# Two reorderings in a two-layer trunk: the sum of the A11 and A12 products behind that of S2, and a tile's square ahead of its multiplication by the norm weights

## The chip, the cores and the metric

The kernel runs on one core of a Trainium2 chip. The metric is the device time of one launch in microseconds; shown are the median, the lowest and the highest of three runs. One more execution is recorded by the hardware profiler, and everything that is read from a trace comes from that one. TensorE is called PE here, VectorE DVE, ScalarE ACT, GpSimd POOL, and SyncE, which issues the transfers of this kernel, SP. Each engine works through its own list of instructions in order; between engines, semaphores make an instruction wait.

## The reference

`x` is 1024 tokens by 1024 features in float32. There are two layers, each with a mixer and a feed-forward block, each normed before and after:

```
for layer in range(2):
    h = rmsnorm(x, norm_mix_pre[layer])
    m = attention_mixer(h, ...) if layer == 0 else recurrent_mixer(h, ...)   # both end in "... @ w_out"
    x = x + rmsnorm(m, norm_mix_post[layer])
    h = rmsnorm(x, norm_ffn_pre[layer])
    f = (silu(h @ w_gate) * (h @ w_up)) @ w_down          # 1024 -> 2816 -> 1024
    x = x + rmsnorm(f, norm_ffn_post[layer])

rmsnorm(x, g) = x * rsqrt(mean(x * x) + 1e-6) * g
```

The change touches two places: the products of `h` with `w_gate` and `w_up`, and the norm of `m` behind the mixer's output product.

## The kernel before, in words

Every float32 operand is split into a high part (a cast, done by ACT) and a low part (the operand less its high part, done by DVE). A product is made of three matmuls: high by high, high by low, low by high.

**Stages.** Attention runs up to 512 us of the profiled execution, its output product (`out_product`) to 609, the gate and up products of layer 0 (`gate_up`) to 1044, its down product to 1268, the recurrent mixer to 1492, its output product to 1589, `gate_up` of layer 1 to 2024, and the down product to the end.

**Gate and up.** Each product by 256 weight columns is a block, done in the Strassen-Winograd way with seven products of half size, A11, A12, S2, S3, S1, S4 and A22 in this order on PE. Each is 12 matmuls of 128x512 (three for each of four 128-row parts), so a block is 84. Eleven gate blocks and eleven up blocks alternate in each layer (the first half of the first gate block runs inside the output product's end). `strassen` writes one block. Its sums come from PSUM: P1 (the A11 product) is copied to SBUF by ACT (L651); then DVE adds the A12 product to it (L653, the output tile c11), the S2 product to it (L654, u2), the S3 product to u2 (L655, u3), the S1 product to u2 and to u3 (L657, L659), the S4 product to u2 (L660), and subtracts the A22 product (L661). Products take turns on six PSUM tiles, each taking the one that is freed first, and so on into the next block: the A22 product takes the tile that P1's copy frees, and the first, second and third product of the next block take those that the first, second and third sum of this one free (L653, L654, L655). So a sum that is late on DVE makes PE wait some products later.

**Loading the weights.** `gate_load` brings the weights of one block in two tiles called `raw`, of 512 KB each: the A half (a11 and a21) and the B half (a12 and a22). There are three `raw` tiles, so a half can only be asked for (L599, on SP's queue) when the half three before it has been read for the last time. For the A half that last reading is the low part of S4 of the load two before; for the B half it is the low part of S3 of the load just before. ACT scales a half by the norm's weights (L602, four pieces of 128x256); then A11, A12 and A22 are split (cast L614 on ACT, low part L615 on DVE), DVE forms S2, S1, S3 and S4 in place (L621, L622, L623, L628), and these are split too. After a gate block ACT applies the silu (L693); after an up block DVE multiplies the two and forms sums for the down product (L698 to L704), which SP stores (L707).

**The output product's norm.** `out_product` treats the 1024 tokens as eight tiles, three, three and two at a time, and leaves each result in PSUM, 128 by 1024. `post_norm_of` then multiplies it by the norm weights into SBUF (DVE, L248), squares and sums it (ACT, L178), lets POOL form the reciprocal root (L182, L183), and DVE adds to the residual (L254). Behind that comes the next norm: a square of `x` (ACT, L178), two steps on POOL, a scaling (ACT, L212), and eight transposes on PE (L222), whose results are split into the operand `hS` of the gate and up products. The last two tiles, 6 and 7, end inside the first gate products. ACT and DVE read the same PSUM tile, and the framework lets one of them wait for the other, in the order of the program text.

**What sets the order.** The framework simulates the program with its own costs before it is built, and fixes each engine's list by that. The text of the kernel gives dependences and priorities, not the list itself; a line that is moved can reorder instructions well away from it.

Of the kernel before, what the change touches and what calls it, by code (L numbers as in the profile page):

```python
# [12 lines left out]
ALU = mybir.AluOpType  # L13
# [14 lines left out]
def rows(t, x):  # L28

    if not isinstance(t, tuple):  # L30
        return [(slice(0, P), x[t * P:(t + 1) * P, :])]
    r, a = t
    o = [2 * a * P + k * P + 64 * r for k in range(2)]
    return [(slice(64 * k, 64 * k + 64), x[o[k]:o[k] + 64, :]) for k in range(2)]
# [65 lines left out]
class Trunk:  # L100
# [134 lines left out]
    def post_norm_of(self, ms, mg, x_src, x_dst, t, gpost, sink, pool, x=None):  # L235

        nc = self.nc
        if x is None:  # L240
            x = pool.tile([P, D], F32, tag="nx", bufs=2, name=self.uid("x"))
        for d, s in rows(t, x_src):
            self.load(x[d, :], s)
        junk = pool.tile([P, D // len(ms)], BF16, tag="junk", bufs=1, name=self.uid("junk"))
        if mg is ms[0][1]:
            rs = self.rstd(pool, [m for _, m in ms], junk)
        for c, m in ms:
            scaled = nc.vector.tensor_tensor(mg[:, c], m, gpost[:, c], op=ALU.mult).ins  # L248
        if mg is not ms[0][1]:
            rs = self.rstd(pool, [m for _, m in ms], junk)  # L250
        self.last_m = [self.squared, scaled]

        def rest(later=False):
            nc.vector.scalar_tensor_tensor(x, mg, rs, x, op0=ALU.mult, op1=ALU.add)  # L254
            for k, (d, s) in enumerate(rows(t, x_dst)):
                (nc.scalar if k and sink is None else nc.sync).dma_start(s, x[d, :])
            if sink is not None:
                return self.pre_norm(pool, x, mg, None, sink, t, self.psum_t, later)

        return rest  # L260
# [211 lines left out]
    def psum(self):  # L472
        return self.pp.tile([P, 512], F32, tag="mm", bufs=6, name=self.uid("ps"))
# [158 lines left out]
    def strassen(self, hS, psum, c, q, cols, behind=()):  # L632

        nc = self.nc
        c11, u2, u3, c22 = c

        def product(name, i):
            ps, a = psum(), q[name]  # L640
            for kt in range(4):
                bh, bl = hS.op(i, 0, kt, cols), hS.op(i, 1, kt, cols)
                with self.behind(behind):
                    nc.tensor.matmul(ps, a[:, 0, kt, :], bh, start=kt == 0, stop=False)  # L644
                nc.tensor.matmul(ps, a[:, 0, kt, :], bl, start=False, stop=False)  # L645
                self.matmul = nc.tensor.matmul(ps, a[:, 1, kt, :], bh, start=False, stop=kt == 3).ins  # L646
            return ps

        tt = nc.vector.tensor_tensor
        p1 = c22  # L650
        nc.scalar.copy(p1, product("A11", 0))  # L651
        yield self.matmul
        tt(c11, product("A12", 1), p1, op=ALU.add)  # L653
        tt(u2, product("S2", 4), p1, op=ALU.add)  # L654
        tt(u3, product("S3", 5), u2, op=ALU.add)  # L655
        p5 = product("S1", 3)
        tt(u2, p5, u2, op=ALU.add)  # L657
        yield self.matmul
        tt(c22, p5, u3, op=ALU.add)  # L659
        tt(u2, product("S4", 2), u2, op=ALU.add)  # L660
        tt(u3, u3, product("A22", 6), op=ALU.subtract)  # L661

    def gate_up(self, ap, hS, early, wg, wu, gain, gO):
# [17 lines left out]
        for j in range(NF // 2):  # L681
            if j == 0:
                cg = blocks()
                strassen([o[:, late] for o in cg], q, late)
                for i, o in enumerate(cg):
                    nc.scalar.activation(o[:, early], first[:, i], AF.Silu)
                    nc.scalar.activation(o[:, late], o[:, late], AF.Silu)
            else:
                q = self.gate_load(ap, wg, gain, j, ["w"] * 7, self.last if j == 1 else None)
                cg = blocks()  # L690
                strassen(cg, q, full)
                for o in cg:
                    nc.scalar.activation(o, o, AF.Silu)  # L693
            qu = self.gate_load(ap, wu, gain, j, ["w"] + ["w2"] * 6, hS.last if j == 0 else None)
            cu = blocks()
            strassen(cu, qu, full)
            for o, u in zip(cg, cu):
                tt(o, u, o, op=ALU.mult)  # L698
            a11, a21, a12, a22 = cg
            s1, s2, s4, _ = cu  # L700
            tt(s1, a21, a22, op=ALU.add)
            tt(a21, a11, a21, op=ALU.subtract)
            tt(s2, s1, a11, op=ALU.subtract)
            tt(s4, a12, s2, op=ALU.subtract)  # L704
            for name, o in (("A11", a11), ("S2", s2), ("S3", a21), ("S1", s1), ("A22", a22),
                            ("S4", s4), ("A12", a12)):
                nc.sync.dma_start(gO[name][:, j] if name == "A12" else gO[name][j], o)  # L707
# [419 lines left out]
```

## Time and profile before

| | us |
|---|---|
| median of three runs | 2259.44 |
| lowest and highest | 2258.71, 2262.77 |
| profiled execution, its own time | 2258.71 |
| span of its trace | 2256.9 |
| PE busy | 2205.0 |
| DVE busy | 1547.2 |
| ACT busy | 1143.2 |
| POOL busy | 227.6 |

The granted TensorE clock was 0.994 of full speed on average. How to read rows: `L615 DVE TENSOR_TENSOR q<-raw,q` is a DVE instruction of kernel line 615 that writes a tile named `q` from tiles named `raw` and `q`; "[4.01 <-ACT q L614]" says that its engine stood idle for 4.01 us before it, and that the last thing it waited for was ACT's line 614. SPq is SP's queue; a row there is the time at which a transfer was issued, not how long it took. PE's records overlap: the duration of a matmul is longer than the distance to the next one.

### The profile page before, as it was taken

The numbers are of one execution on the slowest core, as the hardware profiler recorded it, in microseconds if no ns is written. First come the engines' busy times: TensorE is split into PE (matmuls) and PEld (weight loads), VectorE is DVE, ScalarE is ACT, GpSimd is POOL, SyncE is SP. The second block draws the span as 40 slices with busy tenths as digits, with TensorE's granted clock in tenths as the row PEclk, the third lists the DMA queues.
The fourth block names the chain that finished last, engine by engine and source line by source line (L and its number), as shares of the span: only waits on it lengthen the run. The fifth ranks groups of instructions, "written<-read, shape, count | busy, mean of one in ns | idle before, by whom it ended". The sixth has DMA issues, their size and how long they took to land. (4 is left out here: it accounts for less than half of the span.)

```text
span 2256.9 us, 30747 instructions
## 1 busy us (share of the span) xinstructions
PE 2205.0 (98%) x11198; PEld 1806.0 (80%) x11198; DVE 1547.2 (69%) x2496; ACT 1143.2 (51%) x2108; POOL 227.6 (10%) x458
## 2 busy tenths in 40 slices
PE   8999999999999999999999999999999999999997
PEld 8887888878788887778887777887788887788875
DVE  5776765464877767676867677437777667669665
ACT  4545455465765444442536676538754443425433
POOL 2111212131100000000001233102000000000011
PEclk9999999999999999999999999999999999999998
DMA  5101011125423323226558421356243322337466
GB/s 166 48 29 34 24 43 46 54 98 184 170 85 98 117 94 104 92 97 227 173 157 261 132 65 39 106 189 227 66 131 94 117 87 92 102 127 270 131 202 189
DMA packets 185977, 268.92 MB, mean 119 GB/s; under 512 B 13793, under 2 KB 115169, under 8 KB 185826
## 3 DMA queue, kind: packets, MB, share of 16 engines
q1 hardware_dynamic: 185186, 264.86, 37.3%
q10 hardware_dynamic: 640, 2.10, 0.3%
q8 instruction: 88, 1.44, 0.3%
q14 instruction: 63, 0.52, 0.1%
HBM read 201.38 MB, written 65.54 MB: 118 GB/s over the span
## 5 line engine op out<-in xcount | busy, mean ns | idle before, releaser
L644 PE MATMUL ps<-hS,q 128*128 128x512 f32 (+1 forms) x1288 | 492.8, 383 | 9.1 <-DVE c L655 4.3
L645 PE MATMUL ps<-hS,q 128*128 128x512 f32 (+1 forms) x1288 | 489.5, 380 | 1.4 <-DVE hS L89 1.4
L646 PE MATMUL ps<-hS,q 128*128 128x512 f32 (+1 forms) x1288 | 488.5, 380 | 0.0
L615 DVE TENSOR_TENSOR q<-raw,q 128x512 fp32r<-128x512 f32 x308 | 207.9, 687 | 206.7 <-ACT q L614 205.7
L644 PEld LDWEIGHTS ps<-hS,q 128*128 128x128 f32 x1288 | 241.7, 188 | 66.5 <-DVE c L659 8.1
L645 PEld LDWEIGHTS ps<-hS,q 128*128 128x128 f32 x1288 | 242.3, 188 | 47.2 <-DVE hS L89 1.8
L646 PEld LDWEIGHTS ps<-hS,q 128*128 128x128 f32 x1288 | 242.2, 188 | 46.3
L602 ACT ACTIVATE raw<-raw,gcol 128x256 f32<-128x256 f32 x352 | 151.9, 499 | 207.2 <-DMA raw<-in_ffn_w_gate_dram 95.0
L614 ACT CAST q<-raw 128x512 fp32r<-128x512 f32 x308 | 176.8, 614 | 147.9 <-DVE raw L623 145.0
L730 PE MATMUL ps<-o,o 128*128 128x512 f32 x616 | 241.8, 393 | 2.6 <-DVE o L725 2.6
L731 PE MATMUL ps<-o,o 128*128 128x512 f32 x616 | 239.4, 393 | 0.0
L729 PE MATMUL ps<-o,o 128*128 128x512 f32 x616 | 221.6, 394 | 9.4 <-ACT o L840 7.4
L724 ACT CAST o<-raw 128x512 fp32r<-128x512 f32 x206 | 123.2, 620 | 187.4 <-PE ps L731 54.3
L182 POOL TENSOR_SCALAR rs<-ss 128x1 f32<-128x1 f32 x60 | 34.8, 581 | 1468.5 <-ACT junk L178 1401.7
L725 DVE TENSOR_TENSOR o<-raw,o 128x512 fp32r<-128x512 f32 x206 | 137.6, 687 | 61.6 <-ACT o L724 60.8
L729 PEld LDWEIGHTS ps<-o,o 128*128 128x128 f32 x616 | 116.1, 189 | 38.0 <-ACT o L840 9.9
L156 DVE TENSOR_TENSOR wlo<-raw,whi 128x1024 fp32r<-128x1024 f32 x76 | 93.0, 1224 | 71.3 <-ACT whi L155 70.4
L730 PEld LDWEIGHTS ps<-o,o 128*128 128x128 f32 x616 | 116.7, 189 | 28.3 <-DVE o L725 4.3
L731 PEld LDWEIGHTS ps<-o,o 128*128 128x128 f32 x616 | 116.8, 190 | 25.0 <-DVE o L841 0.9
L155 ACT CAST whi<-raw 128x1024 fp32r<-128x1024 f32 x76 | 79.7, 1050 | 57.1 <-PE ps L167 20.2
L399 ACT COPY pt<-tr 128x512 f32<-128x512 f32 (+1 forms) x128 | 65.5, 527 | 79.6 <-PE tr L395 79.0
L166 PE MATMUL psq<-hT,whi 128*128 128x512 f32 x256 | 101.2, 395 | 1.1 <-DVE v L294 1.1
(201 smaller groups left out, 4306.8 us busy)
## 6 DMA issues: line engine op xcount, KB each, us to landing
raw<-in_ffn_w_down_dram SPq DMA_DIRECT2D x96, 256.0 KB, 4.4
raw<-in_ffn_w_gate_dram SPq DMA_DIRECT2D x44, 512.0 KB, 4.2
raw<-in_ffn_w_up_dram SPq DMA_DIRECT2D x44, 512.0 KB, 3.9
gS<-c SPq DMA_DIRECT2D x88, 256.0 KB, 2.3
raw<-gS SPq DMA_DIRECT2D x88, 256.0 KB, 2.8
gA<-c SPq DMA_DIRECT2D x66, 256.0 KB, 2.9
raw<-in_attn_w_in_dram SPq DMA_DIRECT2D x24, 512.0 KB, 4.1
raw<-gA SPq DMA_DIRECT2D x44, 256.0 KB, 2.7
```

The lines of the kernel that those rows point to most:

```text
L166: nc.tensor.matmul(ps, wh[:, kt, cols], hh[:, kt, :], start=kt == 0, stop=False)
L602: nc.scalar.activation(raw[:, i], raw[:, i], AF.Copy, scale=gain[:, 4 * k + i:4 * k + i + 1])
L614: self.last = nc.scalar.copy(t[:, 0], src).ins
L615: self.last_lo = nc.vector.tensor_tensor(t[:, 1], src, t[:, 0].bitcast(F32), op=ALU.subtract).ins
L644: nc.tensor.matmul(ps, a[:, 0, kt, :], bh, start=kt == 0, stop=False)
L645: nc.tensor.matmul(ps, a[:, 0, kt, :], bl, start=False, stop=False)
L646: self.matmul = nc.tensor.matmul(ps, a[:, 1, kt, :], bh, start=False, stop=kt == 3).ins
L724: nc.scalar.copy(t[:, 0], src)
L725: tt(t[:, 1], src, t[:, 0].bitcast(F32), op=ALU.subtract)
L729: nc.tensor.matmul(ps, a[0], b[:, 0], start=first, stop=False)
L730: nc.tensor.matmul(ps, a[0], b[:, 1], start=False, stop=False)
L731: nc.tensor.matmul(ps, a[1], b[:, 0], start=False, stop=last)
```

## The change

In `strassen`, the tile of P1 is now the one that becomes c11 (now called `s1`), no longer that of c22. The sum u2 of the S2 product and P1 is written first; the sum of the A12 product and P1 follows behind it, in place. In `post_norm_of`, where a tile comes in one part, the square now stands ahead of the multiplication; of the two readers of the PSUM tile, the multiplication is now the one that comes second.

```diff
@@ post_norm_of
-        if mg is ms[0][1]:
+
+        squares_first = mg is ms[0][1] or len(ms) == 1
+        if squares_first:
             rs = self.rstd(pool, [m for _, m in ms], junk)
         for c, m in ms:
             scaled = nc.vector.tensor_tensor(mg[:, c], m, gpost[:, c], op=ALU.mult).ins
-        if mg is not ms[0][1]:
+        if not squares_first:
             rs = self.rstd(pool, [m for _, m in ms], junk)
@@ strassen
-        c11, u2, u3, c22 = c
+        s1, u2, u3, c22 = c
...
         tt = nc.vector.tensor_tensor
-        p1 = c22
-        nc.scalar.copy(p1, product("A11", 0))
+        nc.scalar.copy(s1, product("A11", 0))
         yield self.matmul
-        tt(c11, product("A12", 1), p1, op=ALU.add)
-        tt(u2, product("S2", 4), p1, op=ALU.add)
+        p2 = product("A12", 1)
+        tt(u2, product("S2", 4), s1, op=ALU.add)
+        tt(s1, p2, s1, op=ALU.add)
         tt(u3, product("S3", 5), u2, op=ALU.add)
```

Lines behind the first edit are two further down in the changed kernel: the cast is L616, the low part L617, the scaling L604. Behind the second edit u2 is L655, s1 L656, u3 L657.

The fixed lists of the engines differ in more than these lines. First ACT's list in layer 0, over the stretch that the prediction reads from 941 to 961 us. Before: `raw_9579` and `raw_9585` are the A and the B half of a load; `q_9447` to `q_9453` are the seven operands of the load ahead of it, `q_9448` its A12, `q_9453` its A22, `q_9451` its S1, `q_9452` its S4.

```order
L614 CAST q_9448<-raw_9441 128x512
L693 ACTIVATE c_9173<-c_9173 128x512
L602 ACTIVATE raw_9579<-raw_9579,gcol 128x256 x4
L614 CAST q_9453<-raw_9441 128x512
L614 CAST q_9449<-raw_9435 128x512
L614 CAST q_9450<-raw_9435 128x512
L693 ACTIVATE c_9176<-c_9176 128x512
L614 CAST q_9451<-raw_9441 128x512
L693 ACTIVATE c_9174<-c_9174 128x512
L602 ACTIVATE raw_9585<-raw_9585,gcol 128x256 x2
L614 CAST q_9452<-raw_9441 128x512
```

Of the change, the same place:

```order
L604 ACTIVATE raw_9579<-raw_9579,gcol 128x256 x4
L616 CAST q_9448<-raw_9441 128x512
L616 CAST q_9453<-raw_9441 128x512
L695 ACTIVATE c_9173<-c_9173 128x512
L616 CAST q_9449<-raw_9435 128x512
L616 CAST q_9450<-raw_9435 128x512
L695 ACTIVATE c_9176<-c_9176 128x512
L616 CAST q_9451<-raw_9441 128x512
L695 ACTIVATE c_9174<-c_9174 128x512
L616 CAST q_9452<-raw_9441 128x512
L604 ACTIVATE raw_9585<-raw_9585,gcol 128x256 x4
```

The cast of S4 (`q_9452`) moved from behind the first two pieces of the B half's scaling to ahead of it; the cast of A12 (`q_9448`) moved from ahead of the A half's scaling to behind it.

DVE's list at the same place, before (`c_9173` to `c_9176` are the block's four output tiles):

```order
L615 TENSOR_TENSOR q_9447<-raw_9435,q_9447 128x512
L653 TENSOR_TENSOR c_9173<-ps_9191,c_9176 128x512
L615 TENSOR_TENSOR q_9448<-raw_9441,q_9448 128x512
L654 TENSOR_TENSOR c_9174<-ps_9205,c_9176 128x512
L615 TENSOR_TENSOR q_9453<-raw_9441,q_9453 128x512
L621 TENSOR_TENSOR raw_9441<-raw_9435,raw_9441 128x4x128
L622 TENSOR_TENSOR raw_9435<-raw_9435 128x4x128
L655 TENSOR_TENSOR c_9175<-ps_9219,c_9174 128x512
L623 TENSOR_TENSOR raw_9435<-raw_9441,raw_9435 128x4x128
L628 TENSOR_TENSOR raw_9441<-raw_9441,raw_9435 128x4x128
```

And of the change:

```order
L617 TENSOR_TENSOR q_9447<-raw_9435,q_9447 128x512
L706 TENSOR_TENSOR c_9020<-c_8876,c_9019 128x512
L617 TENSOR_TENSOR q_9448<-raw_9441,q_9448 128x512
L655 TENSOR_TENSOR c_9174<-ps_9204,c_9173 128x512
L617 TENSOR_TENSOR q_9453<-raw_9441,q_9453 128x512
L656 TENSOR_TENSOR c_9173<-ps_9191,c_9173 128x512
L623 TENSOR_TENSOR raw_9441<-raw_9435,raw_9441 128x4x128
L657 TENSOR_TENSOR c_9175<-ps_9219,c_9174 128x512
L624 TENSOR_TENSOR raw_9435<-raw_9435 128x4x128
L625 TENSOR_TENSOR raw_9435<-raw_9441,raw_9435 128x4x128
L630 TENSOR_TENSOR raw_9441<-raw_9441,raw_9435 128x4x128
```

The first sum from PSUM moved from between A11's and A12's low parts (L653) to behind A12's (L655, u2); the sum of P1 and the A12 product (L656) now stands behind A22's low part. In the change the first product of the next block waits for u2 (L655), the second for s1 (L656), the third for u3 (L657). On SP's list the transfer of the A half, `raw_9579`, moved from behind the stores of three of an up block's results to ahead of them.

Last, DVE's list at the norm of tile 6 in layer 0 (`ps_6380` is the tile in PSUM, `mg_6478` its product with the weights, `x_6479` the residual), before:

```order
L89 TENSOR_TENSOR hS_5639<-mg_6285,hS_5638 128x4x64
L248 TENSOR_TENSOR mg_6478<-ps_6380,g_5889 128x1024
L628 TENSOR_TENSOR raw_6510<-raw_6510,raw_6504 128x4x128
L89 TENSOR_TENSOR hS_5641<-tf_6338,hS_5640 128x16x64
L615 TENSOR_TENSOR q_6520<-raw_6504,q_6520 128x512
L89 TENSOR_TENSOR tf_6369<-mg_6285 128x256 x2
L254 SCALAR_TENSOR_TENSOR x_6479<-mg_6478,rs_6483,x_6479 128x1024
```

And of the change:

```order
L250 TENSOR_TENSOR mg_6478<-ps_6380,g_5889 128x1024
L630 TENSOR_TENSOR raw_6510<-raw_6510,raw_6504 128x4x128
L89 TENSOR_TENSOR hS_5641<-tf_6338,hS_5640 128x16x64
L256 SCALAR_TENSOR_TENSOR x_6479<-mg_6478,rs_6482,x_6479 128x1024
L617 TENSOR_TENSOR q_6520<-raw_6504,q_6520 128x512
L617 TENSOR_TENSOR q_6521<-raw_6510,q_6521 128x512
L89 TENSOR_TENSOR tf_6369<-mg_6285 128x256 x2
```

The addition to the residual moved ahead of a low part and of two copies; on ACT the square of this tile moved ahead of the cast of `hS` that it stood behind.

## The prediction

> **What bounds the kernel now.** I read the page's busy times first, then the busy times cut into four stretches (columns: length, busy time and number of instructions of each engine).
>
> ```profile
> PE 2205.0 (98%) x11198; PEld 1806.0 (80%) x11198; DVE 1547.2 (69%) x2496; ACT 1143.2 (51%) x2108; POOL 227.6 (10%) x458
> 640.00:868.00 228.00, 228.00 (x1008) 188.85 (x1007) 166.50 (x267) 111.81 (x230) 0.00 (x0) 1.00 0.35 109
> 868.00:1043.00 175.00, 170.68 (x736) 136.66 (x735) 122.25 (x194) 71.09 (x142) 0.00 (x0) 1.00 0.31 98
> 1621.00:1852.00 231.00, 231.00 (x1021) 191.25 (x1019) 170.41 (x273) 112.36 (x231) 0.00 (x0) 1.00 0.35 107
> 1852.00:2023.00 171.00, 166.63 (x719) 133.64 (x718) 117.70 (x187) 69.98 (x140) 0.00 (x0) 1.00 0.31 100
> ```
>
> These stretches are the gate and up products of the two feed-forward blocks, each cut where PE begins to stall. In the first part of each, a matmul takes 228/1008 = 0.2262 us; in the second 175/736 and 171/719 = 0.2378, at the same granted clock of 1.00. PE therefore loses 175 - 736 x 0.2262 = 8.5 us in layer 0 and 171 - 719 x 0.2262 = 8.4 in layer 1: **16.9 us**, although PE looks 98% busy (a stream of 0.39 us records hides short gaps). A block of seven products, 84 matmuls, needs 19.0 us of PE, and a gate block and an up block together 38.0.
>
> The chain that ended last names what is behind it: its first four entries are loads of `raw`, DVE's low parts and ACT's scaling.
>
> ```profile
> by line: DMA raw<-in_ffn_w_up_dram 2.4%; DVE q L615 2.3%; ACT raw L602 2.1%; DMA raw<-in_ffn_w_gate_dram 2.0%; PE ps L729 1.8%; PE ps L730 1.8%; PE ps L731 1.8%; issue 1.4%; PE ps L644 0.9%; PE ps L645 0.9%; PE ps L646 0.9%; ACT q L614 0.8%
> ```
>
> One turn of that loop, from the timelines of SP's queue, ACT and DVE (columns: start, duration, work, idle time before it and its releaser):
>
> ```profile
> 900.82 0.38 SPq L599 DMA_DIRECT2D raw<-in_ffn_w_up_dram  x1
> 919.92 0.38 SPq L599 DMA_DIRECT2D raw<-in_ffn_w_gate_dram  x1
> 941.18 0.38 SPq L599 DMA_DIRECT2D raw<-in_ffn_w_up_dram  x1
> 954.77 0.38 SPq L599 DMA_DIRECT2D raw<-in_ffn_w_up_dram  x1
> 960.94 0.38 SPq L599 DMA_DIRECT2D raw<-in_ffn_w_gate_dram  x1
> ...
> 945.92 1.71 ACT L602 ACTIVATE raw<-raw,gcol 128x256 f32<-128x256 f32 x4 [2.29 <-DMA raw<-in_ffn_w_up_dram]
> 947.54 0.60 ACT L614 CAST q<-raw 128x512 fp32r<-128x512 f32 x1
> 954.72 0.60 ACT L614 CAST q<-raw 128x512 fp32r<-128x512 f32 x1
> 955.38 0.63 ACT L693 ACTIVATE c<-c 128x512 f32<-128x512 f32 x1
> 958.77 0.91 ACT L602 ACTIVATE raw<-raw,gcol 128x256 f32<-128x256 f32 x2 [2.76 <-DMA raw<-in_ffn_w_up_dram]
> 959.59 0.60 ACT L614 CAST q<-raw 128x512 fp32r<-128x512 f32 x1
> ...
> 948.17 0.69 DVE L615 TENSOR_TENSOR q<-raw,q 128x512 fp32r<-128x512 f32 x1 [4.01 <-ACT q L614]
> 951.55 0.69 DVE L628 TENSOR_TENSOR raw<-raw,raw 128x512 f32<-128x512 f32 x1
> 955.35 0.69 DVE L615 TENSOR_TENSOR q<-raw,q 128x512 fp32r<-128x512 f32 x1
> 955.96 0.68 DVE L661 TENSOR_TENSOR c<-c,ps 128x512 f32<-128x512 f32 x1
> 960.22 0.69 DVE L615 TENSOR_TENSOR q<-raw,q 128x512 fp32r<-128x512 f32 x1 [3.58 <-ACT q L614]
> ```
>
> The A half of a load is asked for at 941.18. ACT scales it at 945.92 and only then casts A22 of the load before (947.54), because that cast stands behind the scaling in ACT's order; DVE waits 4.01 us. S3's low part frees a `raw` tile, and the B half is asked for at 954.77. ACT scales two pieces of it (958.77), then casts S4 (959.59), whose input was ready at 952.2 (L628). DVE waits 3.58, forms the low part, and frees the next `raw` tile: A of the following load at 960.94. Each load thus holds **two DMA round trips in series**. From 900.82 to 941.18 one up block and one gate block take 40.36 us, 2.3 more than PE needs.
>
> PE pays late, because DVE starts with slack:
>
> ```profile
> 635.05 0.40 PE L644 MATMUL ps<-hS,q 128*128 128x512 f32 x1
> 647.96 0.68 DVE L655 TENSOR_TENSOR c<-ps,c 128x512 f32<-128x512 f32 x1
> ...
> 924.39 0.39 PE L644 MATMUL ps<-hS,q 128*128 128x512 f32 x1
> 950.23 0.68 DVE L655 TENSOR_TENSOR c<-ps,c 128x512 f32<-128x512 f32 x1
> 950.97 0.50 PE L644 MATMUL ps<-hS,q 128*128 128x512 f32 x1 [0.97 <-DVE c L655]
> ```
>
> From a block's first matmul to the end of its u3 sum (L655) it is 13.6 us in the first full block and 26.5 in this one, where PE waits for it. The products take six PSUM tiles in turn, so L655, the third sum, frees the one for the third product of the next block, which is due nine products of 2.72 us, 24.5, after this block's start.
>
> **The change, feed-forward part.** No work is added or taken away: the same additions, casts and transfers, in another order; one `c` tile holds P1 and then the A11+A12 sum. What moves is the scheduler's order, in three ways.
>
> Removed: S4's cast no longer stands behind the scaling of B. In this up block it could follow S1's cast and L693, at about 956.0, and its low part L661, at about 956.6 (DVE's starts lie 0.61 apart at 955.35 and 955.96). The next A is then asked for at 957.3 instead of 960.94: 3.6 us. In the gate block DVE is filled longer:
>
> ```profile
> 977.87 0.68 DVE L661 TENSOR_TENSOR c<-c,ps 128x512 f32<-128x512 f32 x1
> 981.22 0.69 DVE L615 TENSOR_TENSOR q<-raw,q 128x512 fp32r<-128x512 f32 x1 [0.86 <-ACT q L614]
> ```
>
> Here the low part can follow L661 at 978.5: 2.7 us. Together 6.3 per pair of blocks.
>
> Added: A12's cast now stands behind the scaling of the next load's A, as A22's did. Behind its landing come one more cast and, on DVE, A12's low part and the s1 sum ahead of A22's combinations. Bounds: 1.2 us (two DVE steps of 0.6; the cast hidden) and 2.4 (two casts or waits of 0.6 more) per load; I take 2.0, since cast and low part follow one another, so 4.0 per pair. SP's queue also moves A ahead of three stores; that lets A go no later than before, and I cost it at nothing: 941.18 to 945.92, 4.7 us, is already the landing of a load with a store issued behind it. Should A land 1 us later beside the stores, that is 2 us per pair, the case called half way below. The stores are read only by the down product, after the last block.
>
> The loop becomes 40.36 - 6.3 + 4.0 = **38.1 us per pair** (bounds 36.5 to 38.9) against PE's 38.0.
>
> The third way costs slack. The first sum after P1 is now u2, behind the S2 product, and it releases the first product of the next block. That is due seven products, 19.0 us, after the block's start, against the 24.5 of the sum that PE waits for now, and u2 stands behind A12's low part, so behind the DMA landing. The slack is some 4 to 5 us, if u2 ends in the early blocks about a microsecond behind the 13.6 us of today's third sum. A loop at 38.1 hardly uses it. At 38.9, 0.45 per block, it lasts ten of 21 blocks, and the rest lose about 5 us in each layer. I take 0.75 us of stall per layer: **-15.4 us** (16.9 - 1.5), with 16.9 and 7 as bounds.
>
> **The change, norm part.** `out_product` squares a tile straight from PSUM; today the square waits for the multiplication by gains on DVE. For the last two tiles of layer 0, PE at the transposes, then tile 6 on DVE, ACT and POOL:
>
> ```profile
> 611.88 1.09 PE L222 MATMUL pst<-ident,mg 128*128 128x128 f32 x8 [1.21 <-ACT mg L212]
> 619.78 1.09 PE L222 MATMUL pst<-ident,mg 128*128 128x128 f32 x8 [1.05 <-ACT mg L212]
> ...
> 602.92 1.21 DVE L248 TENSOR_TENSOR mg<-ps,g 128x1024 f32<-128x1024 f32 x1
> 607.10 1.28 DVE L254 SCALAR_TENSOR_TENSOR x<-mg,rs,x 128x1024 f32<-128x1024 f32 x1
> ...
> 604.17 1.02 ACT L178 ACTIVATE junk<-ps 128x1024 bf16<-128x1024 f32 x1 [1.03 <-DVE mg L248]
> ...
> 606.03 0.90 POOL L183 TENSOR_TENSOR rs<-rs,neghalf 128x1 f32<-128x1 f32 x1
> ```
>
> The square at 604.17 could start about 603.1, when ACT is free; the multiplication then lies beside POOL's two steps. L254 moves from 607.10 to about 606.1, as DVE still has the multiplication and two other steps ahead of it: 1.0 us of tile 6's 1.21. Tile 7 gains a like amount. A third wait per layer, at tile 5, stays, since ACT is busy without a break there.
>
> The Trainium skill, PSUM — Partial Sum Buffer, section "PSUM bank collisions raise a hardware error", says that ScalarE and VectorE must not read one bank at once, even two reads. By it the change swaps which of the two waits and cannot overlap them; the 1.03 us wait above agrees, and the sum is unchanged.
>
> ```profile
> PE pst L222 <- ACT mg L212: 7.6, 6, 1.8
> ```
>
> The six waits hold 7.6 us, so the bounds are 0 and 7.6; below nothing too, since the multiplication now ends a square (1.02 us) later and holds its PSUM tile as long, which would cost up to that much at a place where the next group of tiles waits for it. I take 2 tiles x 2 layers x 0.9 = **-3.5**.
>
> Sum, against the profiled execution's own 2258.71 us (span 2256.9; the median of the three runs is 2259.44): 2258.7 - 15.4 - 3.5 = 2239.8, **2240 us**.
>
> **Rivals.** *Half way*: A12's cast and u2 behind the landing cost more, and the loop runs at 39.2 per pair, 0.6 per block over PE. Slack of 4.5 lasts 8 blocks, the other 13 lose 0.6 each, 7.8 a layer: 16.9 - 15.6 = 1.3 gained, with the norms 4.8: 2254. For it: the 4.01 us wait at 948.17 is not removed. Against: 6.3 us of waiting is taken out in places that the rows name.
>
> *Slower*: the early release decides. If the loop stays at 40.36 because A's round trip and the scaling alone fill it, PE stalls as soon as DVE lags 19.0 instead of 24.5: 5.5 us more in each layer, 2258.7 + 11 - 3.5 = 2266. It decides from a loop of about 39.5 per pair. For it: u2 now stands behind a DMA; against: S4's cast has had its input for 7 us when it runs.
>
> *Nothing*: PE at 98% is the bound, ACT and DVE have time to spare, so reordering them moves no end: 2258. The Trainium skill, Perfetto Trace Analysis, section "Identifying the Most-Contended Engine", would have the engine of highest occupancy optimized first, and by occupancy that is PE. Against: 0.2378 against 0.2262 us per matmul at the same clock.
>
> **How the numbers follow.** Chances: forecast 0.63, half way 0.15, nothing 0.08, slower 0.14. Low end of the range: all 16.9 and most of the 7.6, and 2 more left to chance: 2232. High end: 2259, so that half way and nothing are inside and only the slower case is outside; the forecast's own range is 2233 to 2249. Under 0.2%, 4.5 us, a measurement of this kernel cannot be told from no change. Forecast and half way mostly lie beyond it (0.78), nothing inside (0.08), slower beyond (0.14).
>
> **What would show it.** Right: matmuls at 0.226 us up to the end of both stretches; DVE's low parts waiting about 3.6 us once per load, not twice; A loads 38.0 apart per pair, set by PE; the square's wait on DVE gone, a wait of DVE's multiplication on ACT in its place. Wrong: PE waiting for u2 (L655 of the changed program) from the middle of the stretch on, or A loads still 40 us apart per pair.

## The result

| | before | changed |
|---|---|---|
| median, us | 2260.9 (four runs beside the change) | 2241.1 |
| lowest to highest, us | 2258.71 to 2262.77 | 2236.41 to 2243.03 |
| profiled execution, span, us | 2256.9 | 2239.6 |

The ratio is 0.991, with a 95% interval of 0.9891 to 0.9929: the changed kernel is faster by 0.9%, some 20 us. Repeated later, beside other runs of the kernel before (median 2256.93 us), it took 2239.87 us, 0.9929 (0.9915 to 0.9942). The forecast was 2240 us.

The same cut of the busy times, for the changed kernel (columns: length, then busy time and instructions of PE, its weight loads, DVE, ACT, POOL, the granted clock, the DMA share, GB/s):

```profile
640.00:868.00 228.00, 228.00 (x1007) 188.81 (x1006) 170.90 (x276) 113.88 (x233) 0.00 (x0) 1.00 0.35 111
868.00:1036.00 168.00, 168.00 (x743) 139.09 (x742) 116.21 (x187) 68.61 (x136) 0.00 (x0) 1.00 0.32 104
1612.00:1852.00 240.00, 240.00 (x1061) 198.79 (x1060) 178.70 (x290) 121.40 (x250) 0.00 (x0) 1.00 0.34 109
1852.00:2010.00 158.00, 158.00 (x699) 130.88 (x698) 110.11 (x178) 62.08 (x122) 0.00 (x0) 1.00 0.34 107
```

A matmul now takes 168/743 = 0.2261 and 158/699 = 0.2260 us in the second parts, as in the first parts. The stalls of 16.9 us are gone, all of them. DVE has the same work, and PE's share of the span is 98% as before: the page's first lines do not tell the two kernels apart.

One turn of the loop in the changed kernel, from the timelines of SP's queue, ACT and DVE:

```profile
923.76 0.38 SPq L601 DMA_DIRECT2D raw<-in_ffn_w_up_dram  x1
938.67 0.38 SPq L601 DMA_DIRECT2D raw<-in_ffn_w_up_dram  x1
941.17 0.38 SPq L601 DMA_DIRECT2D raw<-in_ffn_w_gate_dram  x1
956.79 0.37 SPq L601 DMA_DIRECT2D raw<-in_ffn_w_gate_dram  x1
960.99 0.38 SPq L601 DMA_DIRECT2D raw<-in_ffn_w_up_dram  x1
...
939.81 0.60 ACT L616 CAST q<-raw 128x512 fp32r<-128x512 f32 x1
942.76 1.71 ACT L604 ACTIVATE raw<-raw,gcol 128x256 f32<-128x256 f32 x4 [2.35 <-DMA raw<-in_ffn_w_up_dram]
...
926.45 0.69 DVE L617 TENSOR_TENSOR q<-raw,q 128x512 fp32r<-128x512 f32 x1 [0.91 <-ACT q L616]
930.50 0.69 DVE L617 TENSOR_TENSOR q<-raw,q 128x512 fp32r<-128x512 f32 x1 [2.75 <-ACT q L616]
940.45 0.69 DVE L617 TENSOR_TENSOR q<-raw,q 128x512 fp32r<-128x512 f32 x1
946.01 0.69 DVE L617 TENSOR_TENSOR q<-raw,q 128x512 fp32r<-128x512 f32 x1 [4.88 <-ACT q L616]
948.14 0.69 DVE L617 TENSOR_TENSOR q<-raw,q 128x512 fp32r<-128x512 f32 x1 [1.43 <-ACT q L616]
```

The B half is asked for at 938.67 and scaled at 942.76. S4's cast no longer waits for that: it runs at 939.81, its low part at 940.45, and the next A half is asked for at 941.17, 2.5 us behind the B half instead of the 6.2 of before (954.77 to 960.94). DVE no longer waits ahead of S4's low part, where it waited 3.58 us; its waits for casts that follow a landing stay, 0.91 and 2.75 us for one load, 4.88 and 1.43 for the other. From 923.76 to 960.99 a pair of blocks takes 37.2 us; before it took 40.36. (The five pairs from 773.57 to 960.99 average 37.5.) The raw loads have left the head of the chain that ended last, which now runs over the matmuls of the gate and up products (L646 to L648).

Stage by stage, from the matmuls that begin each stage in the trace (the output product from the second of its eight row steps), in us. One execution of e2 took 3112 us at a granted clock of 0.65 and is left out of all comparisons.

| | before | changed | feed-forward part alone (e1) | norm part alone (e2) | norm part for tiles 0 to 5 (e7) |
|---|---|---|---|---|---|
| output product, layer 0 | 92.4 | 90.9 | 92.9 | 90.8 | 90.8 |
| gate and up, layer 0 | 434.9 | 426.5 | 425.9 | 434.8 | 426.0 |
| down, layer 0 | 224.8 | 226.7 | 224.7 | 224.5 | 226.2 |
| output product, layer 1 | 92.9 | 90.9 | 92.9 | 90.8 | 90.8 |
| gate and up, layer 1 | 434.7 | 427.0 | 425.0 | 433.1 | 426.0 |

The changed kernel wins 16.0 us in the gate and up stages and 3.4 in the output products. It loses 1.9 in layer 0's down product, which the change does not touch, and each of the rest moves by less than 1 us: 17.3 us of span. In the second profile of the same kernel that down product took 224.3 us, so the 1.9 belongs to that execution (e7's two profiles differ there in the same way, 226.2 and 224.1).

### The profile page after: what moved, and what is told of

Same layout as the page of the kernel before. It is cut to its first block, busy times and chain, and to the rows that moved or that the text cites. A ratio compares the mean times of both kernels' runs of the same rounds, so it can differ in the third digit from the quotient of the medians.

```text
span 2239.6 us, 30733 instructions
## 1 busy us (share of the span) xinstructions
PE 2194.9 (98%) x11198; PEld 1806.9 (81%) x11198; DVE 1539.4 (69%) x2496; ACT 1146.0 (51%) x2108; POOL 227.3 (10%) x458
## 3 DMA queue, kind: packets, MB, share of 16 engines
q1 hardware_dynamic: 185186, 264.86, 37.5%
## 5 line engine op out<-in xcount | busy, mean ns | idle before, releaser
L646 PE MATMUL ps<-hS,q 128*128 128x512 f32 (+1 forms) x1288 | 489.7, 381 | 0.7 <-ACT hS L96 0.3
L647 PE MATMUL ps<-hS,q 128*128 128x512 f32 (+1 forms) x1288 | 489.0, 380 | 0.9 <-DVE hS L89 0.9
L648 PE MATMUL ps<-hS,q 128*128 128x512 f32 (+1 forms) x1288 | 488.4, 380 | 0.0
L617 DVE TENSOR_TENSOR q<-raw,q 128x512 fp32r<-128x512 f32 x308 | 204.5, 685 | 185.7 <-ACT q L616 185.2
L647 PEld LDWEIGHTS ps<-hS,q 128*128 128x128 f32 x1288 | 242.1, 188 | 47.5 <-DVE hS L89 1.3
L646 PEld LDWEIGHTS ps<-hS,q 128*128 128x128 f32 x1288 | 241.7, 188 | 47.8 <-ACT hS L96 0.7
L648 PEld LDWEIGHTS ps<-hS,q 128*128 128x128 f32 x1288 | 242.1, 188 | 45.8
L616 ACT CAST q<-raw 128x512 fp32r<-128x512 f32 x308 | 177.3, 616 | 154.7 <-DVE raw L625 127.6
L604 ACT ACTIVATE raw<-raw,gcol 128x256 f32<-128x256 f32 x352 | 150.2, 498 | 151.8 <-DMA raw<-in_ffn_w_up_dram 73.2
L182 POOL TENSOR_SCALAR rs<-ss 128x1 f32<-128x1 f32 x60 | 33.1, 551 | 1451.5 <-ACT junk L178 1367.8
L731 PEld LDWEIGHTS ps<-o,o 128*128 128x128 f32 x616 | 116.2, 189 | 38.9 <-ACT o L842 8.5
```

The source lines that it names most:

```text
L604: nc.scalar.activation(raw[:, i], raw[:, i], AF.Copy, scale=gain[:, 4 * k + i:4 * k + i + 1])
L616: self.last = nc.scalar.copy(t[:, 0], src).ins
L617: self.last_lo = nc.vector.tensor_tensor(t[:, 1], src, t[:, 0].bitcast(F32), op=ALU.subtract).ins
L731: nc.tensor.matmul(ps, a[0], b[:, 0], start=first, stop=False)
```

## The experiments

**Each part alone.** e1 has the diff's `strassen` part only, e2 its `post_norm_of` part only.

> The feed-forward part alone, the norm as before. Theory (two DMA round trips in series per load, of which the change takes one out): PE's 17 us of stalls in the two gate and up stretches go, so 2260.9 - 17 = about 2244 (2241 to 2246), matmuls at 0.226 us in all four stretches. Rival (the norm part feeds the loop an earlier start and does a good share): no more than 10 us gained, 2251 or above.

> The norm part alone, the sums of the products as before. As the prediction had it: 3.5 us gained, 2257.4, all of it at the waits before the transposes of tiles 6 and 7. As the trace of the changed kernel reads: 2 to 3 us, because the wait at tile 5 (1.27 and 1.77 us) goes and those at tiles 6 and 7 do not shrink as a sum. In both the gate and up stretches keep their 17 us of stalls, and DVE's lag starts later by as much as PE comes earlier, so a rival says nothing is gained: what PE wins at the norm it waits for at the end of the stretch, 2260 to 2261.

e1: 2238.45 us beside 2257.6, ratio 0.9911 (0.9895 to 0.9926). This is the whole gain; the rival, which gave the norm a good share of it, is out. e2: 2257.1 us (median of ten), 0.9994 (0.9983 to 1.0005), no difference that can be measured. Its profile does show output products shorter by about 1.5 and 2 us, and PE waiting less ahead of the transposes (all waits of PE on ACT's L212, first in e1, then in e2; columns: total, times, longest):

```profile
PE pst L222 <- ACT mg L212: 7.4, 6, 1.8
```

```profile
PE pst L222 <- ACT mg L212: 4.9, 4, 2.0
PE ps L646 <- DVE c L657: 3.7, 7, 0.8
```

The second row of e2 is part of the stalls on the sums (here on the third, L657), still there. Two of the six waits are gone, those at tile 5; but of those left the ones at tile 6 are longer than any before.

**The order on ACT alone.** e3 is the kernel before, with the scaling of a B half held behind the S4 cast of the load before:

```diff
@@ gate_load
+        s4 = getattr(self, "s4", None)
         for k in range(2):
...
-            with self.tc.issue_after(after) if after else nullcontext():
+            with ExitStack() as st:
+                for o in (after, s4 if k else None):
+                    if o:
+                        st.enter_context(self.tc.issue_after(o))
                 for i in range(4):
...
             split("S4", a12)
+        self.s4 = self.last
         return q
```

e4 is the kernel before with the u2 sum written first, and P1 left in c22's tile:

```diff
@@ strassen
-        tt(c11, product("A12", 1), p1, op=ALU.add)
+        p2 = product("A12", 1)
         tt(u2, product("S2", 4), p1, op=ALU.add)
+        tt(c11, p2, p1, op=ALU.add)
```

> The kernel before with one order added: the scaling of a load's B half is held behind the cast of S4 of the load before on ACT. The sums keep their order, A12's cast stays ahead of the scaling of A, the norm is as before. Theory: this placement alone is what the feed-forward part gains by, so PE's stalls go: 2244 (2241 to 2247), and A loads come 38 us apart per pair, set by PE. Rival (the order of the sums and the tile that they free do it): 2259 to 2262.

> The kernel before with the u2 sum written ahead of the A11 + A12 sum, P1 still in the tile of c22. ACT's list has S4's cast ahead of the scaling of B here too. Theory: 2244, as the feed-forward part, since the tile of P1 does not matter. Rival (P1 must leave the tile of c22, which is written late): 2250 or more, with PE waiting for c tiles.

e3: 2240.29 us, 0.9922 (0.9904 to 0.9941). e4: 2241.81 us, 0.9925 (0.9912 to 0.9939). Both lie where the feed-forward part lies, within the noise, and both rivals are out. The second parts of e3's stretches:

```profile
868.00:1036.00 168.00, 168.00 (x743) 139.16 (x742) 117.44 (x184) 69.12 (x136) 0.00 (x0) 1.00 0.32 101
1852.00:2005.00 153.00, 153.00 (x677) 126.73 (x676) 106.47 (x165) 62.22 (x120) 0.00 (x0) 1.00 0.33 104
```

0.2261 and 0.2260 us per matmul again, with the sums in their old order. So the change's lines are not needed for the gain: written that way, they lead the scheduler to put one cast ahead of a scaling that waits for a transfer. e4's trace has that order of the two as well, so the sums' order is enough to bring it about; no difference from the tile of P1 can be told.

e3's edit adds one order, but the scheduler moved more with it: A12's cast stands behind the scaling of A in every second block (the expectation had it stay ahead), and on SP's list the A half's transfer moved ahead of stores, as in the change. Neither explains the gain. A12's cast is a cost in the prediction's sum, and SP's place did not set the time: in both kernels the A half is asked for 0.03 us after S4's low part ends (before, 960.22 + 0.69 = 960.91 and 960.94; changed, 941.14 and 941.17). The opposite test, the changed sums with the cast left behind the scaling, was not run.

**How much slack is left, and whether the early release has a price.** The slower rival rested on u2 freeing the next block's first product. e5 and e9 load the feed-forward part's loop with idle work on ACT; e6 and e10 load e3's, which has the late release. The idle work is a multiplication by 1.0, which leaves the result as it is (e5 and e6; `4 * 2` in e9 and e10):

```diff
@@ gate_load
+        slow = j >= 1
...
+                for i in range(4 * 1 if slow and k == 0 else 0):
+                    nc.scalar.activation(raw[:, i % 4], raw[:, i % 4], AF.Copy)
                 for i in range(4):
...
```

> The feed-forward part alone, plus 1.7 us of idle work on ACT per load: each A half, from the second block pair on, is multiplied by 1.0 in four pieces ahead of its scaling. In the changed kernel DVE's lag falls by some 0.6 us per block where PE sets the pace, so its loop alone would take about 18.4 us per block; with the extra work 20.1, 1.1 more than PE. Theory of the early release (u2 frees the next block's first product, due at 19.0 us; lag starts at about 13.5): 5.5 us of slack, so 22 x 1.1 - 5.5 = 18.7 us of stalls in each layer, 37 in all: 2276, PE waiting for u2. Rival (which sum comes first does not matter): the same time as the kernel with the late release and the same extra work.

> The kernel before with S4's cast held ahead of the scaling of B, plus the same 1.7 us of idle work on ACT per load. Sums in the old order: the third is due at 24.5 us. Theory: at the same loop of 20.1 us per block it has 11 us of slack, so 22 x 1.1 - 11 = 13 us of stalls in each layer, 26 in all: 2266, some 10 us ahead of the early release. Rival: within 3 us of it.

e5: 2237.63 us, 0.9909 (0.9894 to 0.9923). e6: 2242.23 us, 0.9929 (0.9912 to 0.9945). Both expectations missed by far: 1.7 us more of ACT's work per load, and no stall at all. In e5's trace u2 ends 14 to 16 us after its block's start in nearly every block behind the first five. Where the lag fell by about 0.4 us per block without the idle work (e1, the later blocks), it now stands still, so of the 1.7 us only about 0.4 reached the loop; the rest presumably went into time in which ACT had been waiting. e6 is the slower one by 4.6 us, but not by stalls, as neither has any: its profile has 2.4 us more in the two gate and up stages and 2.3 more from layer 1's down product to the end. Why was not followed.

> As e5, with 3.4 us of idle work on ACT per load instead of 1.7. In e5 the loop just kept PE's pace: u2 ended 15 to 16 us after the start of its block, block after block. With 1.7 us more it must fall behind by up to 1.7 us per block. Theory of the early release: PE stalls from the third or fourth block on, as soon as u2's end passes 19.0 us after its block's start, and it is u2 that it waits for. Blocks then take 20.8 us, about 28 us of stalls in each layer: 2290 or so. Rival: the onset is the old one, with DVE 24 us or more behind at the third sum.

> As e6, with 3.4 us of idle work on ACT per load. In e6 the third sum's end went from 14 to 21 us behind the start of its block over 17 blocks, without a stall. With 1.7 us more per block: about 2 us per block, so the stall begins when the third sum ends 24.5 us after its block's start, five or six blocks in, two to four later than in e9, and PE waits for the third sum (u3). Blocks then take about 21 us; the total is near e9's, since this loop is itself the slower one by 0.3 us per block. Rival: PE stalls at the same block as in e9.

e9: 2243.46 us (two runs), 0.9942 (0.9922 to 0.9961). e10: 2240.22 us (two runs), 0.9927 (0.9908 to 0.9947). The sizes are wrong again, and the onset by some seven blocks in layer 0 and by more in layer 1, but the mechanism shows. In e9 (the sum u2 is L656 there, the first matmul of a block L647):

```profile
803.17 0.39 PE L647 MATMUL ps<-hS,q 128*128 128x512 f32 x1
...
822.52 0.69 DVE L656 TENSOR_TENSOR c<-ps,c 128x512 f32<-128x512 f32 x1
...
823.26 0.50 PE L647 MATMUL ps<-hS,q 128*128 128x512 f32 x1 [0.89 <-DVE c L656]
```

The block begins at 803.17, u2 ends at 823.21, 20.0 us later, and PE, due at 822.2, waits for it. From there on most blocks take 19.2 to 19.5 us in layer 0, where PE needs 19.04. In e10, with the late release (third sum L663):

```profile
958.82 0.39 PE L652 MATMUL ps<-hS,q 128*128 128x512 f32 x1
978.41 0.69 DVE L663 TENSOR_TENSOR c<-ps,c 128x512 f32<-128x512 f32 x1
```

the third sum ends 20.3 us after its block's start, the worst of the layer, and PE loses nothing. So the limit of 19.0 us is real, and the old one is beyond 20.3. In the changed kernel the limit is not reached: u2's worst lag is 15.6 us in layer 0 and 16.5 in layer 1. But it is reached in e1, without any idle work, in three blocks of layer 0 (u2 is L653 there, the first matmul L644):

```profile
767.92 0.50 PE L644 MATMUL ps<-hS,q 128*128 128x512 f32 x1
786.66 0.69 DVE L653 TENSOR_TENSOR c<-ps,c 128x512 f32<-128x512 f32 x1
787.40 0.50 PE L644 MATMUL ps<-hS,q 128*128 128x512 f32 x1
```

Here u2 ends 19.4 us after its block's start, and the next block begins at 787.40 instead of 786.96. With its two neighbours that is 0.7 us. The loop is as fast as the changed kernel's; in e1's first blocks DVE simply fell further behind, and why was not followed. So the early release has a price, small here, and it depends on the lag with which a layer begins as well as on the loop's speed. e10's loop falls behind more slowly than e9's, not faster as expected, so the two totals do not isolate the price of the release; only the place of the stall does.

**Where the norm part gains and loses.** e7 and e8 are e1 with the square first for some tiles only:

```diff
@@ post_norm_of
-        squares_first = mg is ms[0][1] or len(ms) == 1
+        squares_first = mg is ms[0][1] or (len(ms) == 1 and t < 6)      # e7; t >= 6 in e8
```

> The feed-forward part, and the norm part for tiles 0 to 5 only. Theory (what the norm part wins at tile 5 PE waits for at tile 6): the output product gets some 2 us shorter in each layer, tile 6's wait grows from 1.2 to 2.0 us, and the first full block starts less than 1 us earlier than with the feed-forward part alone; the time is that of the feed-forward part within 1 us. As the prediction had it, nothing changes at all, since tile 5's wait was to stay.

> The feed-forward part, and the norm part for tiles 6 and 7 only. As the prediction had it, this is the whole gain of the norm part: the waits at these two tiles (1.2 and 0.7 us here) all but go, 1.8 us per layer, 3.5 in all. Theory from the trace of the changed kernel: tile 6's chain gets about 0.8 us shorter, as its multiplication leaves the chain, and POOL's steps and the place of the next square behind a cast that waits for PE take up the rest; 1 us per layer.

e7: 2235.88 us, 0.9902 (0.9887 to 0.9917), the shortest median of all. e8: 2241.44 us, 0.993 (0.9916 to 0.9945). PE at tile 6's transposes in layer 0, first e7, then e8:

```profile
608.57 1.09 PE L222 MATMUL pst<-ident,mg 128*128 128x128 f32 x8 [1.26 <-ACT mg L212]
```

```profile
612.52 1.70 PE L222 MATMUL pst<-ident,mg 128*128 128x128 f32 x8 [2.45 <-ACT mg L212]
```

Both expectations fail at tile 6. For tiles 0 to 5 the part shortens the output product by 2.0 us per layer, and tile 6's wait stays at 1.26 us rather than growing. From the output product's mark to the first full block e7 takes 116.9 us in both layers, e1 118.1 and 118.0: 1.2 us gained per layer. For tiles 6 and 7 the part takes away tile 7's wait of 0.7 us but makes tile 6's 2.45 us where it was 1.2, and that stretch takes 119.9 and 119.3 us: 1.3 to 1.7 lost against e1. (e3, e4 and e10, with the norm as before, take 119.3 there too, so e1's 118 is itself owed to e1's lists.) ACT's timeline in e8, with POOL's last step for tile 6, shows how:

```profile
606.95 0.62 ACT L616 CAST q<-raw 128x512 fp32r<-128x512 f32 x1 [1.10 <-PE ps L497]
608.02 1.06 ACT L178 ACTIVATE mg<-x 128x1024 f32<-128x1024 f32 x1 [0.45 <-DVE x L256]
610.10 0.37 ACT L652 COPY first<-ps 128x256 f32<-128x256 f32 x1 [0.93 <-PE ps L648]
610.37 1.05 ACT L96 CAST hS<-tf 128x1024 fp32r<-128x1024 f32 x1
611.32 1.15 ACT L212 ACTIVATE mg<-x,rs 128x1024 f32<-128x1024 f32 x1
...
610.02 0.57 POOL L183 TENSOR_TENSOR rs<-rs,neghalf 128x1 f32<-128x1 f32 x1
```

In this list the copy of a product (L652, which waits for PE) and a cast stand ahead of tile 6's scaling (L212), and hold it up by 0.7 us: POOL is done at 610.59. Once more the greater part is a place in a list, not the edited line. The changed kernel has the tiles' parts together: tile 5's wait gone, tile 6's 1.98 us.

e11 and e12 repeat the changed kernel and e7 beside each other.

> The changed kernel again, for a comparison on one chip with the next run: ratio 0.991 to the kernel before.

> The feed-forward part with the norm part for tiles 0 to 5 only, which had the shortest output products. Theory: 1 to 2 us below the changed kernel, since tiles 6 and 7 lose by the norm part; about 0.9903 of the kernel before. Rival: no difference that can be told, within 1 us.

e11: 2239.87 us, 0.9929 (0.9915 to 0.9942). e12: 2236.4 us, 0.9909 (0.9896 to 0.9923). e7's kernel was the shorter one both times, by 3.5 us here, and the intervals just overlap: probably better than the changed kernel, not certainly. The size is more than the 1 to 2 us expected. In both pairs of profiles the stretch from layer 1's down product to the end is 2.3 us shorter in e7's kernel (231.4 and 231.5 us against 233.8 twice), which the expectation did not look at and which was not followed further. In e12's profile the output product of layer 1 took 93.2 us instead of 90.8, so the gain there does not come in every execution.

## Why the prediction was right, and where it was not

**The bound.** Right. The loop of two DMA round trips in series per load was what PE stalled on, and e3 settles it: one order added on ACT, with the sums, the tile of P1 and the norm as before, gives 0.9922. This answers the rival that PE at 98% leaves nothing to win. The Trainium skill, Perfetto Trace Analysis, section "Identifying the Most-Contended Engine", has the busiest engine optimized first; here PE was the busiest and the remedy lay on ACT at 51%, so the distance from matmul to matmul, 0.2378 against 0.2262 us, was the better guide. The same section warns that matmul busy time is a poor measure of how close a kernel is to its limit, and with that this case agrees: 98% before and after.

**The removed wait.** Right: S4's cast stands ahead of the B half's scaling, DVE's wait ahead of S4's low part is gone, and A is asked for 2.5 us behind B. The half-way rival pointed at the wait of 4.01 us for a cast behind A's landing. A wait of that length remains, 4.88 us at 946.01 for a cast behind B's, but it does not make the loop slower than PE.

**The loop's size.** "The loop becomes 38.1 us per pair" was too long. It measured 37.2 in this turn and 37.5 on average, inside the bounds of 36.5 to 38.9 and well short of the half-way rival's 39.2, and e5 and e9 show that it takes 1.7 us more of ACT's work per load before DVE stops catching up. The sign "A loads 38.0 apart per pair, set by PE" did not come: DVE was still catching up. Two more rows of the kernel before give the steps of the same turn there:

```profile
913.95 0.38 SPq L599 DMA_DIRECT2D raw<-in_ffn_w_up_dram  x1
933.91 0.37 SPq L599 DMA_DIRECT2D raw<-in_ffn_w_gate_dram  x1
```

From B to the next A it was 5.97 and 7.27 us and is 2.50 and 4.20: 6.5 removed, where the prediction had 6.3. From A to B it was 13.13 and 13.99 and is 14.91 and 15.62: 3.4 added. The term that was mis-sized is this addition, taken as 4.0 us per pair for A12's cast and what follows it. So the 0.75 us of stall per layer that were left in the sum did not occur in either profile of the changed kernel: the term is 16.9 us, not 15.4. That they were not a mistake in kind is shown by the 0.7 us in layer 0 of e1.

**The slack of the early release.** The slack of 4 to 5 us was a little too large for the early blocks and then grew. In the changed kernel, u2 (L655) against its block's first matmul:

```profile
728.40 0.39 PE L646 MATMUL ps<-hS,q 128*128 128x512 f32 x1
743.25 0.68 DVE L655 TENSOR_TENSOR c<-ps,c 128x512 f32<-128x512 f32 x1
...
956.88 0.39 PE L646 MATMUL ps<-hS,q 128*128 128x512 f32 x1
968.32 0.69 DVE L655 TENSOR_TENSOR c<-ps,c 128x512 f32<-128x512 f32 x1
```

15.5 us in an early block (the worst of layer 0 is 15.6, of layer 1 16.5), 12.1 in a late one, with 19.0 allowed: a slack of 2.5 to 3.5 us where it was least. The slower rival's mechanism exists, as e9 and e1 show; its condition, a loop of about 39.5 us per pair, was far away.

**The norm part.** Wrong in place, and too large. The step that failed is "L254 moves from 607.10 to about 606.1 ... 1.0 us of tile 6's 1.21. Tile 7 gains a like amount. A third wait per layer, at tile 5, stays, since ACT is busy without a break there." Tile 5's wait went: ACT's unbroken stretch there began at 585 us, but in a chain whose squares had waited for DVE. The first and the last square of that group of tiles, in the kernel before and in the changed one:

```profile
579.00 1.02 ACT L178 ACTIVATE junk<-ps 128x1024 bf16<-128x1024 f32 x1 [2.44 <-DVE mg L248]
587.71 1.02 ACT L178 ACTIVATE junk<-ps 128x1024 bf16<-128x1024 f32 x1
```

```profile
577.07 1.02 ACT L178 ACTIVATE junk<-ps 128x1024 bf16<-128x1024 f32 x1 [1.18 <-PE ps L497]
583.15 1.00 ACT L178 ACTIVATE junk<-ps 128x1024 bf16<-128x1024 f32 x1
```

The first starts 1.9 us earlier, 1.2 of it against the start of the output product; the last, that of tile 5, starts 4.6 us earlier and has moved ahead in ACT's list. A stretch without a break should be asked what its head waited for, and whether its order will stay.

At tile 6 the wait rose from 1.21 to 1.98 us, though L254 moved by more than was forecast: it is L256 now and starts at 604.27 instead of 607.10. PE came to the transposes 2.2 us earlier (608.50 instead of 610.67), and of the chain's lead POOL's two steps took back 1.1 us. Before, then changed:

```profile
609.65 0.35 POOL L182 TENSOR_SCALAR rs<-ss 128x1 f32<-128x1 f32 x1 [2.71 <-ACT mg L178]
610.08 0.57 POOL L183 TENSOR_TENSOR rs<-rs,neghalf 128x1 f32<-128x1 f32 x1
```

```profile
604.27 1.28 DVE L256 SCALAR_TENSOR_TENSOR x<-mg,rs,x 128x1024 f32<-128x1024 f32 x1
607.15 1.29 POOL L182 TENSOR_SCALAR rs<-ss 128x1 f32<-128x1 f32 x1 [4.83 <-ACT mg L178]
608.52 0.72 POOL L183 TENSOR_TENSOR rs<-rs,neghalf 128x1 f32<-128x1 f32 x1
...
610.48 1.09 PE L222 MATMUL pst<-ident,mg 128*128 128x128 f32 x8 [1.98 <-ACT mg L212]
618.14 1.09 PE L222 MATMUL pst<-ident,mg 128*128 128x128 f32 x8 [0.51 <-ACT mg L212]
```

POOL's long step is there in both layers, in both profiles of the changed kernel and in e2, so it belongs to this order of the lists. With POOL's steps as short as before, tile 6's wait would be about 0.9 us, an estimate from these rows. Tile 7 gained as forecast in kind, but half as much: its wait fell from 1.05 to 0.51 us, and to 0.81 in layer 1.

For the term of -3.5 us the comparison of e2 with the kernel before gives -1.4 us, with an interval from -3.8 to +1.1, and the changed kernel is no faster than e1: its stretch to the first full block takes 117.6 and 118.0 us, e1's 118.1 and 118.0. That ACT and DVE swap which of them waits on the PSUM tile, and do not overlap, came out as said: in the changed kernel it is DVE's multiplication of tile 7 that waits for ACT's square:

```profile
611.46 1.23 DVE L250 TENSOR_TENSOR mg<-ps,g 128x1024 f32<-128x1024 f32 x1 [2.64 <-ACT junk L178]
```

**The sum.** 2240 against 2241.1; the gain was forecast as 18.9 us and measured as 19.8, and as 17.1 in the repetition. The feed-forward term was 1.5 us too small, the norm term some 2 us too large, and that the two errors cancelled is luck. The total is no proof of the terms; e1 and e2 are.

## What to carry to other kernels

Where engines work through lists in order, look for an instruction whose input has long been ready standing behind one that waits for a transfer: here one cast per load, behind a scaling, cost 17 us in all, on an engine half idle. When a scheduler writes the lists, read them after an edit, since the edit's own lines may matter less than what they displace; and if one placement is the gain, fix that placement by an explicit order. A stall that a change takes out is only won if the next wait in the same chain does not take it back: follow it to the engine that sets the end.

## What was not expected of the hardware

The same POOL instruction on 128 numbers (L182) took 0.22 us at one place of the changed kernel's execution and, as shown above, 1.29 at another. Beside it, on DVE:

```profile
601.45 0.22 POOL L182 TENSOR_SCALAR rs<-ss 128x1 f32<-128x1 f32 x1 [9.09 <-ACT junk L178]
601.39 1.22 DVE L250 TENSOR_TENSOR mg<-ps,g 128x1024 f32<-128x1024 f32 x1
...
607.15 1.29 POOL L182 TENSOR_SCALAR rs<-ss 128x1 f32<-128x1 f32 x1 [4.83 <-ACT mg L178]
607.34 0.68 DVE L617 TENSOR_TENSOR q<-raw,q 128x512 fp32r<-128x512 f32 x1
```

In the first case DVE reads one operand from PSUM, in the second both from SBUF. The two profiles, of the kernel before and of the changed one, hold 128 executions of L182. All 61 that took more than 0.3 us overlap a DVE instruction with both operands in SBUF; the 56 that overlap no such instruction took at most 0.28; the other 11 overlap such an instruction and were short all the same. That is a coincidence in time, not a test: no run moved the DVE instruction away, and the profiler's spans on POOL are rough.
